# The feed-forwards' first products as seven products of quarters (Strassen), on a two-layer encoder trunk

## The chip, the cores and the metric

One core of one Trainium2 chip runs the whole program in one launch. The metric is the device time of one execution in microseconds (us); the kernel before takes 2049.79 us in the median of 3 runs (2049.25 to 2050.43). A profile of a further execution gives busy time, waits and a timeline for each engine: PE (TensorE matmuls; PEld is its weight load), DVE (VectorE), ACT (ScalarE), POOL (GpSimd) and SP (SyncE, which here issues the loads).

## What is computed

512 frames and 16 learned meta tokens (528 rows of 1024 features) pass through an input LayerNorm and two layers. Each layer has a feed-forward, a mixer and a second feed-forward, each followed by a residual sum and a LayerNorm:

```python
def swiglu_ffn(x, w13, w2):
    a, u = jnp.split(x @ w13, 2, axis=-1)
    return (jax.nn.silu(a) * u) @ w2
for l in range(DEPTH):
    h = layer_norm(DEEPNORM_ALPHA * h + 0.5 * swiglu_ffn(h, ffn1_w13[l], ffn1_w2[l]), ln_g[l, 0], ln_b[l, 0])
    mix = token_mix(h, w_in[l], pool_w[l], pool_scale[l], conv_dw[l], conv_db[l], ...)
    h = layer_norm(DEEPNORM_ALPHA * h + mix, ln_g[l, 1], ln_b[l, 1])
    h = layer_norm(DEEPNORM_ALPHA * h + 0.5 * swiglu_ffn(h, ffn2_w13[l], ffn2_w2[l]), ln_g[l, 2], ln_b[l, 2])
return h[:, N_META:]
```

The hidden width is 2752, that is 21 units of 128 columns and a rest of 64; a unit has a tile of `a` weights and a tile of `u` weights, each 1024 x 128. All data are float32.

## The kernel before

Activations lie transposed: 8 tiles of 128 features, each in two halves of 264 rows (256 frames and 8 meta rows; 256 in the last feed-forward), called s = 0 and s = 1. Each product of float32 numbers is made as three matmuls of a shorter format (`mm3`, lines 101 to 105): every operand is split into a high part, which ACT casts, and a low part, which DVE subtracts (`weights`, lines 82 to 92, for weights; `split`, lines 95 to 99, for activations). The low x low product is left out.

The four feed-forwards are called f0a, f0b, f1a and f1b; the mixers m0 and m1 lie behind f0a and f1a. A feed-forward (`ffn`, and `last_ffn` for f1b) goes through three parts of hidden units (`PARTS`, line 54; the rest of 64 has the number 21). In each part it first makes the hidden units (`hidden_part`, `hidden`): for each unit and each half 8 x 2 `mm3`, then ACT's silu and DVE's product with `u`, and a split. Then comes the second product over that part's units: for each of 8 output tiles m and each half one chain of `mm3` into one PSUM bank, and DVE adds the bank to the residual (`residual`, line 308). In the first part the first three units (`AHEAD`) are done for s = 0 first and for s = 1 after that, since the LayerNorm before them ends earlier for s = 0.

The last part runs inside `normed`: `SKEW` = 6 of the 8 tiles are done for s = 0 and later for s = 1, so that the LayerNorm of s = 0 lies beside the second half of the matmuls, and that of s = 1 beside the next stage's matmuls of s = 0.

Every engine has one queue in order, and a scheduler that is part of the framework fixes that order when the program is built; `issue_after` holds some weights behind the LayerNorm. SP issues all weight loads (512 KB for a 128 x 1024 tile). Buffers are rings: 3 raw weight tiles (`RAW`), 7 high and 7 low ones (`WB`). PSUM has 8 banks: 4 `acc`, 2 `att`, 2 `stat`. POOL does low parts of odd activation tiles, some LayerNorm sums and parts of the mixer; it issues no transfer.

Of the kernel before, what the change touches and what calls it, by code (L numbers as in the profile page):

```python
# [16 lines left out]
P = 128  # L17
D = 1024
# [34 lines left out]

PARTS = ([0, 1, 21, 2, 3, 4], list(range(5, 13)), list(range(13, 21)))


def trunk(ctx, tc, a):
# [43 lines left out]
    def mm3(out, w, x, start, stop):  # L101
        (wh, wl), (xh, xl) = w, x
        nc.tensor.matmul(out, lhsT=wh, rhs=xh, start=start, stop=False)  # L103
        nc.tensor.matmul(out, lhsT=wh, rhs=xl, start=False, stop=False)  # L104
        nc.tensor.matmul(out, lhsT=wl, rhs=xh, start=False, stop=stop)  # L105

# [76 lines left out]
    for tt in range(6):  # L183
        y = wp.tile([P, 1024], F32, tag="hi" if tt % 2 else "lo", name=f"xtok{tt}", bufs=WB)
        tok.append(y[: HM if tt >= 4 else P])

    def load_tokens(tts):
        for tt in tts:
            if tt >= 4:
                nc.sync.dma_start(out=tok[tt], in_=a["meta"][(tt - 4) * HM : (tt - 3) * HM, :])  # L190
                continue
            for c in range(0, D, 512):
                sl = slice(c, c + 512)
                nc.sync.dma_start(out=tok[tt][:, sl], in_=a["x"][tt * P : (tt + 1) * P, sl])

# [246 lines left out]
    def mixer(l, name):  # L442
# [507 lines left out]
```

## Time and profile before

| | us |
|---|---|
| median of 3 runs | 2049.79 |
| profiled execution, its own time | 2050.98 |
| its span, first to last instruction | 2049.2 |
| PE busy | 2001.1 |
| DVE busy | 1055.9 |
| ACT busy | 643.4 |
| POOL busy | 194.1 |

The 16 engines that move data are busy 28.5% of the span with SP's queue and move 178 MB. Of the names in the rows, `f0b_9a_r` is the raw tile of the `a` weights of unit 9 in f0b, `_h` and `_l` its high and low parts, `f0b_9p` the PSUM bank of its products, `f0b_y` a bank of the second product, `m_ln`, `f0b_ln` a LayerNorm behind a mixer or behind f0b. A row of a timeline gives the start, the duration, the engine, the line and the operation.

### The profile page before, as it was taken

The numbers are of one execution on the slowest core, as the hardware profiler recorded it, in microseconds if no ns is written. First come the engines' busy times: TensorE is split into PE (matmuls) and PEld (weight loads), VectorE is DVE, ScalarE is ACT, GpSimd is POOL, SyncE is SP. The second block draws the span as 40 slices with busy tenths as digits, with TensorE's granted clock in tenths as the row PEclk, the third lists the DMA queues.
The fourth block names the chain that finished last, engine by engine and source line by source line (L and its number), as shares of the span: only waits on it lengthen the run. The fifth ranks groups of instructions, "written<-read, shape, count | busy, mean of one in ns | idle before, by whom it ended". The sixth has DMA issues, their size and how long they took to land.

```text
span 2049.2 us, 36659 instructions
## 1 busy us (share of the span) xinstructions
PE 2001.1 (98%) x15344; PEld 1924.7 (94%) x15344; DVE 1055.9 (52%) x2450; ACT 643.4 (31%) x1180; POOL 194.1 (9%) x283
## 2 busy tenths in 40 slices
PE   7999999999999999999999999999999999999997
PEld 6999999997899999999999999999888999998996
DVE  7343333589767443333473433336886683433336
ACT  5322223333324422222262222223333253222230
POOL 4000000340003000000120000004300030000001
PEclk9999999999999999999999999999999999999999
DMA  4432322222211343322233333222222123333231
GB/s 150 132 113 85 99 87 83 74 92 80 63 41 43 97 119 95 93 87 90 64 96 89 101 95 94 89 87 75 71 90 63 42 64 102 96 101 102 84 103 42
DMA packets 54118, 177.98 MB, mean 87 GB/s; under 512 B 6192, under 2 KB 10160, under 8 KB 53952
## 3 DMA queue, kind: packets, MB, share of 16 engines
q1 hardware_dynamic: 52800, 174.59, 28.5%
q8 instruction: 120, 1.97, 0.4%
q10 hardware_dynamic: 1152, 1.05, 0.2%
q14 instruction: 46, 0.38, 0.1%
HBM read 173.52 MB, written 2.10 MB: 86 GB/s over the span
## 4 chain that ended last, share of the span: by engine, by line
PE 84%; DVE 9%; POOL 2%; issue 2%; ACT 1%; DVEq 0%; POOLq 0%; ACTq 0%
PE f1a_y L104 2%; PE f0a_y L104 2%; PE f1a_y L105 2%; PE f1bo L764 2%; PE f1bo L766 2%; PE f0a_y L105 2%; PE f1bo L765 2%; PE f0a_y L103 2%; PE f1a_y L103 2%; PE f0b_y L104 2%; PE f0b_y L105 2%; PE f0b_y L103 2%; DVE m0y L486 1%; DVE m1y L486 1%; PE m1o L614 1%
## 5 line engine op out<-in xcount | busy, mean ns | idle before, releaser
L92 DVE TENSOR_TENSOR f1bw_l<-f1bw_r,f1bw_h 128x512 fp32r<-128x512 f32 x42 | 27.9, 685 | 48.0 <-ACT f1bw_h L89 48.0
L92 DVE TENSOR_TENSOR f0b_o_l<-f0b_o_r,f0b_o_h 128x512 fp32r<-128x512 f32 (+1 forms) x48 | 28.6, 618 | 45.1 <-ACT f0b_o_h L89 45.1
L92 DVE TENSOR_TENSOR f1a_o_l<-f1a_o_r,f1a_o_h 128x512 fp32r<-128x512 f32 (+1 forms) x48 | 28.7, 620 | 45.0 <-ACT f1a_o_h L89 45.0
L92 DVE TENSOR_TENSOR f0a_o_l<-f0a_o_r,f0a_o_h 128x512 fp32r<-128x512 f32 (+1 forms) x48 | 28.6, 618 | 44.8 <-ACT f0a_o_h L89 44.8
L486 DVE SCALAR_TENSOR_TENSOR m1y<-m1u,vec,m1y 128x528 f32<-128x528 f32 x60 | 46.7, 814 | 0.1
L486 DVE SCALAR_TENSOR_TENSOR m0y<-m0u,vec,m0y 128x528 f32<-128x528 f32 x60 | 46.6, 814 | 0.1
L89 ACT CAST f0b_o_h<-f0b_o_r 128x1024 fp32r<-128x1024 f32 (+1 forms) x24 | 22.5, 939 | 55.1 <-PE f0b_y L104 15.6
L89 ACT CAST f1a_o_h<-f1a_o_r 128x1024 fp32r<-128x1024 f32 (+1 forms) x24 | 22.5, 939 | 54.9 <-PE f1a_y L104 15.6
L89 ACT CAST f0a_o_h<-f0a_o_r 128x1024 fp32r<-128x1024 f32 (+1 forms) x24 | 22.5, 938 | 54.7 <-PE f0a_y L104 15.6
L825 POOL TENSOR_TENSOR yt<-yt,g_last 128x256 f32<-128x256 f32 x4 | 3.1, 782 | 346.8 <-ACT yt L824 346.8
L89 ACT CAST f1bw_h<-f1bw_r 128x1024 fp32r<-128x1024 f32 (+1 forms) x22 | 22.2, 1007 | 43.8 <-PE f1bo L766 6.9
L308 DVE TENSOR_TENSOR h<-h,f0b_y 128x264 f32<-128x264 f32 x32 | 13.7, 428 | 41.9 <-PE f0b_y L105 41.9
L308 DVE TENSOR_TENSOR x<-x,f0a_y 128x264 f32<-128x264 f32 x32 | 13.7, 428 | 41.7 <-PE f0a_y L105 41.6
L308 DVE TENSOR_TENSOR h<-h,f1a_y 128x264 f32<-128x264 f32 x32 | 13.7, 427 | 41.7 <-PE f1a_y L105 41.5
L251 POOL TENSOR_TENSOR f0b_ln_s<-h,h 128x264 f32<-128x264 f32 x2 | 1.5, 752 | 324.7 <-DVE h L308 324.7
L251 POOL TENSOR_TENSOR f1a_ln_s<-h,h 128x264 f32<-128x264 f32 x2 | 1.5, 754 | 324.1 <-DVE h L308 324.1
L251 POOL TENSOR_TENSOR f0a_ln_s<-x,x 128x264 f32<-128x264 f32 x2 | 1.5, 758 | 322.3 <-DVE x L308 322.3
L770 DVE TENSOR_TENSOR yt<-yt,f1bo 128x256 f32<-128x256 f32 x48 | 17.2, 417 | 24.8 <-PE f1bo L766 24.8
L104 PE MATMUL m0mo<-m0cat_l,m0wo_h 128*128 128x264 f32 x96 | 27.7, 290 | 0.0
L104 PE MATMUL m1mo<-m1cat_l,m1wo_h 128*128 128x256 f32 x96 | 27.6, 288 | 0.0
L103 PE MATMUL m0mo<-m0cat_h,m0wo_h 128*128 128x264 f32 x96 | 27.4, 288 | 0.0
L105 PE MATMUL m0mo<-m0cat_h,m0wo_l 128*128 128x264 f32 x96 | 27.3, 285 | 0.0
(9053 smaller groups left out, 8847.5 us busy)
## 6 DMA issues: line engine op xcount, KB each, us to landing
f1bw_r<-in_w2last SPq DMA_DIRECT2D x20, 512.0 KB, 4.3
f0a_o_r<-in_w SPq DMA_DIRECT2D x16, 512.0 KB, 4.3
f0b_o_r<-in_w SPq DMA_DIRECT2D x16, 512.0 KB, 3.8
f1a_o_r<-in_w SPq DMA_DIRECT2D x16, 512.0 KB, 4.0
m0wo_r<-in_w_out SPq DMA_DIRECT2D x8, 512.0 KB, 3.5
m1wo_r<-in_w_out SPq DMA_DIRECT2D x8, 512.0 KB, 3.5
m0w_r<-in_w_in SPq DMA_DIRECT2D x6, 512.0 KB, 3.6
m1w_r<-in_w_in SPq DMA_DIRECT2D x6, 512.0 KB, 3.6
```

The lines of the kernel that those rows point to most:

```text
L89: nc.scalar.copy(out=hi[:, :n], in_=w[:, :n])
L92: e.tensor_tensor(out=lo[:, sl], in0=w[:, sl], in1=raw(hi[:, sl]), op=ALU.subtract)
L103: nc.tensor.matmul(out, lhsT=wh, rhs=xh, start=start, stop=False)
L104: nc.tensor.matmul(out, lhsT=wh, rhs=xl, start=False, stop=False)
L105: nc.tensor.matmul(out, lhsT=wl, rhs=xh, start=False, stop=stop)
L308: nc.vector.tensor_tensor(out=y, in0=y, in1=ps, op=ALU.add)
L486: nc.vector.scalar_tensor_tensor(out=ys[c], in0=src, scalar=wk, in1=ys[c], op0=ALU.mult, op1=ALU.add)
L614: nc.tensor.matmul(o[:, c0 : c0 + cw], lhsT=v, rhs=sm, start=i == 0, stop=i == len(sms) - 1)
L764: nc.tensor.matmul(o, lhsT=hh, rhs=wh, start=part > 0 and i == 0, stop=False)
L765: nc.tensor.matmul(o, lhsT=hh, rhs=wl, start=False, stop=False)
L766: nc.tensor.matmul(o, lhsT=hl, rhs=wh, start=False, stop=i == nk - 1)
L770: nc.vector.tensor_tensor(out=y[:, :256], in0=y[:, :256], in1=o, op=ALU.add)
```

## The change

Units 2 to 20 of every feed-forward (19 of 22 entries) no longer take 96 matmuls but 84. The operand is taken as quarters: a11, a12 are feature tiles 0 to 3 and 4 to 7 of half s = 0, a21, a22 those of s = 1; b11, b21 are the two halves of the `a` tile, b12, b22 those of the `u` tile. Seven products of 4 `mm3` replace eight. For these,

- `sums` makes four sums of activations, once in a feed-forward (4 x 4 DVE operations of 128 x 264, and 16 splits);
- `sum_weights` makes, for each unit, t3 = b12 + b22 and t1 = b11 + b12 in place in the raw tiles by transfers that POOL issues and that add while they write, then t2 = t1 + b22 and t4 = t2 + b21 on DVE, and splits all seven operands (seven low parts of 128 x 512 on DVE instead of four);
- `hidden_by_sums` runs the products one after another into two banks, P and Q (and R), adding onto what is there; ACT copies a bank out before the next product is added to it, and DVE combines the copies.

The parts become five: units 0, 1, 21, 2, 3; then three parts of four; then five. `RAW` goes from 3 to 4, `WB` from 7 to 5, the tiles of `hc` from 32 to 20; a new ring of 16 `wide` tiles takes the sums of activations, several mixer tiles and the weights of the last output tiles. `normed` gets `SKEW_F` = 8 in the feed-forwards: all 8 tiles of s = 0, then all of s = 1. The LayerNorm of m1 now keeps its result in `h`, which `sums` reads.

```diff
-TILES = {"x": 32, "h": 16, "hc": 32, "g": 4, "r2": 2, "sm": 5, "s": 2, "q": 4, "dg": 2}
+TILES = {"x": 32, "h": 16, "hc": 20, "g": 4, "r2": 2, "sm": 5, "s": 2, "q": 4, "dg": 2}
-RAW, WB = 3, 7
-SKEW, AHEAD = 6, 3
+RAW, WB, YB = 4, 5, 2
+SKEW, SKEW_F, AHEAD = 6, 8, 3
-PARTS = ([0, 1, 21, 2, 3, 4], list(range(5, 13)), list(range(13, 21)))
+PARTS = ([0, 1, 21, 2, 3], *(list(range(u, u + 4)) for u in (4, 8, 12)), list(range(16, 21)))
...
+    def sums(n, name):
+        out = [[], [], [], []]
+        for i in range(KT // 2):
+            (a11, a21), (a12, a22) = ([y[:, :n] for y in h[m]] for m in (i, i + KT // 2))
+            s1, s2, s3, s4 = (t(f"{name}s{j}{i}", "q" if i % 2 else "sm")[:, :n] for j in range(4))
+            nc.vector.tensor_tensor(out=s1, in0=a21, in1=a22, op=ALU.subtract)
+            nc.vector.tensor_tensor(out=s2, in0=s1, in1=a11, op=ALU.subtract)
+            nc.vector.tensor_tensor(out=s3, in0=a11, in1=a21, op=ALU.subtract)
+            nc.vector.tensor_tensor(out=s4, in0=a12, in1=s2, op=ALU.add)
+            for j, y in enumerate((s1, s2, s3, s4)):
+                out[j].append(split_wide(y, n, f"{name}S{j}{i}"))
+        return out
+
+    def half_split(w, hi, lo, c):
+        sl = slice(c, c + 512)
+        nc.scalar.copy(out=hi[:, sl], in_=w)
+        nc.vector.tensor_tensor(out=lo[:, sl], in0=w, in1=raw(hi[:, sl]), op=ALU.subtract)
+
+    def sum_weights(src, name):
...
+        nc.sync.dma_start(out=wa, in_=src[0])
+        nc.sync.dma_start(out=wu, in_=src[1])
+        b11, b21, b12, b22 = wa[:, :512], wa[:, 512:], wu[:, :512], wu[:, 512:]
+        add = lambda o, y: nc.vector.tensor_tensor(out=o, in0=o, in1=y, op=ALU.add)
+        A, X, U, Y = pair("a"), pair("x"), pair("u"), pair("y", 512, YB)
+        nc.scalar.copy(out=A[0], in_=wa)
+        for c in (0, 512):
+            nc.vector.tensor_tensor(out=A[1][:, c : c + 512], in0=wa[:, c : c + 512], in1=raw(A[0][:, c : c + 512]), op=ALU.subtract)
+        nc.gpsimd.dma_start(out=b12, in_=src[1][:, 512:], accum_op=ALU.add)
+        nc.gpsimd.dma_start(out=b11, in_=src[1][:, :512], accum_op=ALU.add)
+        half_split(b11, *X, 0)
+        nc.scalar.copy(out=U[0], in_=wu)
+        add(b11, b22)
+        half_split(b11, *X, 512)
+        for c in (0, 512):
+            nc.vector.tensor_tensor(out=U[1][:, c : c + 512], in0=wu[:, c : c + 512], in1=raw(U[0][:, c : c + 512]), op=ALU.subtract)
+        add(b21, b11)
+        half_split(b21, *Y, 0)
...
+    def hidden_by_sums(w, S, n, name):
...
+        product(p_, a11, b11, True)
+        m1 = copy(p_, "m1")
+        product(r_, a12, b21, True)
+        nc.vector.tensor_tensor(out=m1, in0=r_[:, :n], in1=m1, op=ALU.add)
+        g0 = t(f"{name}g0", "g")[:, :n]
+        nc.scalar.activation(g0, m1, AF.Silu)
+        product(p_, s2, t2, False)
+        u2 = copy(p_, "u2")
+        product(q_, s1, t1, True)
+        m5 = copy(q_, "m5")
+        product(p_, s3, t3, False)
+        u3 = copy(p_, "u3")
+        nc.vector.tensor_tensor(out=m5, in0=m5, in1=u3, op=ALU.subtract)
+        product(q_, s4, b22, False)
+        nc.vector.tensor_tensor(out=u2, in0=q_[:, :n], in1=u2, op=ALU.subtract)
+        first = gated(g0, u2, 0)
+        product(p_, a22, t4, False)
...
-                normed(KT, step, ns, v, f"{name}_ln", i == 1)
+                normed(KT, step, ns, v, f"{name}_ln", i == 1, SKEW_F)
...
-        normed(KT, step, no, V_LN + (3 * l + 1) * 16, f"{name}_ln", not last)
+        normed(KT, step, no, V_LN + (3 * l + 1) * 16, f"{name}_ln", True, SKEW)
```

Three places of the new order matter below. The first is DVE's queue in f0b where the three plain units (0, 1, 21) end and unit 2 begins. `21h` is the hidden tile of entry 21, `bS` a low part of a sum of activations, `2a` the weights of unit 2. Before:

```order
913 L92 TENSOR_TENSOR f0b_2a_l<-f0b_2a_r,f0b_2a_h 128x512 [waits DMAHW3_49]
914 L291 TENSOR_TENSOR m_ln_x4l<-h_1_7225,m_ln_x4h 128x264 [waits Activation_49]
915 L92 TENSOR_TENSOR f0b_2a_l<-f0b_2a_r,f0b_2a_h 128x512
916 L92 TENSOR_TENSOR f0b_2u_l<-f0b_2u_r,f0b_2u_h 128x512 [waits DMAHW4_49]
917 L92 TENSOR_TENSOR f0b_2u_l<-f0b_2u_r,f0b_2u_h 128x512
918 L291 TENSOR_TENSOR m_ln_x6l<-h_1_7281,m_ln_x6h 128x264 [waits Activation_49]
919 L363 SCALAR_TENSOR_TENSOR f0b_21h_7622<-f0b_21p_0_7596,f0b_21g_7621 64x264 [waits PE_49,Activation_49]
```

Now (`2x` holds t1 and t2 of unit 2, L427 are the two additions, a wait on a name with DMASW is for a transfer of POOL):

```order
1175 L390 SCALAR_TENSOR_TENSOR f0b_21h_8238<-f0b_21p_0_8212,f0b_21g_8237 64x264
1176 L127 TENSOR_TENSOR f0bS_8324<-f0bs_8310,f0bS_8324 128x264 [waits Activation_49]
1177 L431 TENSOR_TENSOR f0b_2a_lo<-f0b_2a_r,f0b_2a_hi 128x512 [waits DMAHW5_49]
1178 L117 TENSOR_TENSOR f0b_21x_l<-f0b_21h_8238,f0b_21x_h 128x264 [waits Activation_49]
1179 L431 TENSOR_TENSOR f0b_2a_lo<-f0b_2a_r,f0b_2a_hi 128x512
1180 L468 TENSOR_TENSOR f0b_2m_8370<-f0b_2R,f0b_2m_8370 128x264 [waits PE_49,Activation_49]
1181 L416 TENSOR_TENSOR f0b_2x_lo<-f0b_2a_r,f0b_2x_hi 128x512 [waits DMASW0_49,Activation_49]
1182 L427 TENSOR_TENSOR f0b_2a_r<-f0b_2a_r,f0b_2u_r 128x512 [waits DMAHW6_49,DVE_49]
1183 L439 TENSOR_TENSOR f0b_2u_lo<-f0b_2u_r,f0b_2u_hi 128x512 [waits DMASW6_49,Activation_49]
1184 L439 TENSOR_TENSOR f0b_2u_lo<-f0b_2u_r,f0b_2u_hi 128x512
1185 L427 TENSOR_TENSOR f0b_2a_r<-f0b_2a_r 128x512 [waits DVE_49]
1186 L416 TENSOR_TENSOR f0b_2x_lo<-f0b_2a_r,f0b_2x_hi 128x512 [waits Activation_49]
```

The low part of unit 2's weights stood ahead of the first product of entry 21 with its gate; now it stands behind all sums and behind the last gate of entry 21.

The second place is ACT's queue while PE does unit 12 of f0b, the first unit of a part. L458 copies a bank out (`12m` from P, then `12u` from P, then `12m` from Q).

```order
777 L429 CAST f0b_13a_hi<-f0b_13a_r 128x1024 [waits DMAHW5_49,PE_49,Activation_49]
778 L415 CAST f0b_12y_hi<-f0b_12a_r 128x512 [waits DVE_49]
779 L458 COPY f0b_12m_10626<-f0b_12P 128x264 [waits PE_49]
780 L415 CAST f0b_13x_hi<-f0b_13a_r 128x512 [waits DMASW5_49,Activation_49]
781 L435 CAST f0b_13u_hi<-f0b_13u_r 128x1024 [waits DMASW3_49,DMAHW6_49,PE_49,Activation_49]
782 L470 ACTIVATE f0b_12g_10641<-f0b_12m_10626 128x264 [waits DVE_49]
783 L458 COPY f0b_12u_10655<-f0b_12P 128x264 [waits PE_49]
784 L415 CAST f0b_13x_hi<-f0b_13a_r 128x512 [waits DVE_49]
785 L429 CAST f0b_14a_hi<-f0b_14a_r 128x1024 [waits DMAHW7_49,PE_49,Activation_49]
786 L458 COPY f0b_12m_10669<-f0b_12Q 128x264 [waits PE_49]
```

Four casts of later units' weights now stand among the copies on which PE's next additions to P and Q wait; before, casts stood there too, but no bank was wanted back within a unit.

The third place is DVE's queue at the same time (`h_1` is the residual of the second product that ends just before unit 12):

```order
1418 L431 TENSOR_TENSOR f0b_13a_lo<-f0b_13a_r,f0b_13a_hi 128x512 [waits DMAHW5_49,Activation_49]
1419 L416 TENSOR_TENSOR f0b_12y_lo<-f0b_12a_r,f0b_12y_hi 128x512 [waits Activation_49]
1420 L335 TENSOR_TENSOR h_1_7776<-h_1_7776,f0b_y_7_1_10569 128x264 [waits PE_49]
1421 L431 TENSOR_TENSOR f0b_13a_lo<-f0b_13a_r,f0b_13a_hi 128x512
1422 L468 TENSOR_TENSOR f0b_12m_10626<-f0b_12R,f0b_12m_10626 128x264 [waits PE_49,Activation_49]
```

The second low part of unit 13's weights, after which POOL may start the adding transfer into b11 of unit 13, stands behind the last residual of the stage before.

## Rows read from the trace of the kernel before

**Rows 1.** The page: busy time of each engine, and granted TensorE clock in 40 slices.
```profile
PE 2001.1 (98%) x15344; PEld 1924.7 (94%) x15344; DVE 1055.9 (52%) x2450; ACT 643.4 (31%) x1180; POOL 194.1 (9%) x283
...
PEclk9999999999999999999999999999999999999999
```
**Rows 2.** Waits of PE: tile, line, what it waited for: us in total, times, longest.
```profile
PE tr L230 <- DVE xtok L215: 11.2, 1, 11.2
...
PE m0sc L595 <- DVE m0sm L606: 4.8, 1, 4.8
...
PE f0b_0p L104 <- DVE m_ln_x6l L291: 1.0, 1, 1.0
```
**Rows 3.** Matmuls of four units: ns min/median/max, then first and last start in us.
```profile
L103 PE MATMUL f0a_5p<-x_h,f0a_5a_h x16: 279/284/286, 122.9 to 133.8; 128*128 128x264 f32 x16
...
L103 PE MATMUL f0a_6p<-x_h,f0a_6a_h x16: 279/284/286, 134.5 to 145.5; 128*128 128x264 f32 x16
...
L103 PE MATMUL f1b_9p<-m_ln_x0h,f1b_9a_h x2: 281/281/281, 1811.3 to 1817.0; 128*128 128x256 f32 x2
...
L103 PE MATMUL f1b_10p<-m_ln_x0h,f1b_10a_h x2: 281/281/281, 1822.6 to 1828.3; 128*128 128x256 f32 x2
```
**Rows 4.** Windows: length, busy us of PE, PEld, DVE, ACT, POOL, clock, DMA share, GB/s.
```profile
495.00:500.00 5.00, 3.64 (x16) 3.65 (x17) 5.00 (x12) 0.06 (x1) 2.21 (x2) 0.50 0.00 0
...
666.00:683.00 17.00, 15.97 (x128) 15.52 (x127) 13.76 (x26) 10.89 (x23) 3.50 (x4) 1.00 0.52 157
766.00:778.00 12.00, 12.00 (x100) 12.00 (x99) 4.32 (x9) 3.40 (x6) 0.00 (x0) 1.00 0.31 89
```
**Rows 5.** Timeline of DVE at the start of f0b: start, us, instruction, count.
```profile
652.30 2.80 DVE L262 TENSOR_TENSOR h<-h,m_ln_mean 128x264 f32<-128x264 f32 x8 [1.23 <-PE m_ln_mean L256]
...
671.04 1.28 DVE L92 TENSOR_TENSOR f0b_2u_l<-f0b_2u_r,f0b_2u_h 128x512 fp32r<-128x512 f32 x2
672.24 0.98 DVE L291 TENSOR_TENSOR m_ln_x6l<-h,m_ln_x6h 128x264 fp32r<-128x264 f32 x1
...
681.64 0.43 DVE L369 SCALAR_TENSOR_TENSOR f0b_1g<-f0b_1p,f0b_1g 128x264 f32<-128x264 f32 x1
```
**Rows 6.** Timeline of ACT at the start of f0b.
```profile
649.63 1.03 ACT L89 CAST f0b_2u_h<-f0b_2u_r 128x1024 fp32r<-128x1024 f32 x1
650.57 0.41 ACT L285 CAST m_ln_x3h<-h 128x264 fp32r<-128x264 f32 x1
...
668.93 0.40 ACT L285 CAST m_ln_x5h<-h 128x264 fp32r<-128x264 f32 x1
669.23 0.52 ACT L288 ACTIVATE m_ln_x6h<-h,vec 128x264 fp32r<-128x264 f32 x1
```
**Rows 7.** Timeline of PE where unit 2 of f0b begins.
```profile
683.17 0.28 PE L103 MATMUL f0b_2p<-m_ln_x0h,f0b_2a_h 128*128 128x264 f32 x1
```
**Rows 8.** DMA issues: KB each, median us from issue to landing.
```profile
m0wo_r<-in_w_out SPq DMA_DIRECT2D x8, 512.0 KB, 3.5
...
f0b_o_r<-in_w SPq DMA_DIRECT2D x8, 320.0 KB, 3.0
...
xtok<-in_x SPq DMA_DIRECT2D x8, 256.0 KB, 5.9
...
out<-yt SPq DMA_DIRECT2D x8, 128.0 KB, 1.8
```
**Rows 9.** Timeline of PE behind the wait in m0.
```profile
496.36 0.79 PE L595 MATMUL m0sc<-m0q00r,m0k00r 128*128 128x128 f32 x2 [4.80 <-DVE m0sm L606]
...
497.17 0.42 PE L104 MATMUL m0gp<-f0a_ln_x2l,m0wg_h 128*128 128x264 f32 x1
497.39 0.42 PE L105 MATMUL m0gp<-f0a_ln_x2h,m0wg_l 128*128 128x264 f32 x1
```
**Rows 10.** Timeline of DVE in f0b's LayerNorm of s = 0: last residual, first scaled tile.
```profile
1015.38 0.43 DVE L308 TENSOR_TENSOR h<-h,f0b_y 128x264 f32<-128x264 f32 x1 [2.49 <-PE f0b_y L105]
...
1031.41 2.09 DVE L281 SCALAR_TENSOR_TENSOR h<-h,vec,f0b_ln_rs 128x264 f32<-128x264 f32 x5 [0.47 <-PE f0b_ln_rs L171]
```

More of the change, by code (lines that the diff above doesn't have):

```diff
@@ L93, in weights, with weights_wide, tile_of @@
         return hi, lo
+    def weights_wide(src, n, name):
+        w = wp.tile([P, 1024], F32, tag="raw", name=f"{name}_r", bufs=RAW)
+        nc.sync.dma_start(out=w[:, :n], in_=src)
+        out = []
+        for c in range(0, n, 512):
+            k = min(512, n - c)
+            hi, lo = (wide(f"{name}_{p_}{c}", F32R) for p_ in "hl")
+            nc.scalar.copy(out=hi[:, :k], in_=w[:, c : c + k])
+            nc.vector.tensor_tensor(out=lo[:, :k], in0=w[:, c : c + k], in1=raw(hi[:, :k]), op=ALU.subtract)
+            out.append((hi, lo))
+        return out
+    def tile_of(w, j):
+        if isinstance(w, list):
+            return at(w[j // 4], slice(j % 4 * P, (j % 4 + 1) * P))
+        return at(w, slice(j * P, (j + 1) * P))
     def split(src, n, name, tag="hc"):
@@ L99, in split, with wide, split_wide, mm3 @@
         return hi, lo
-    def mm3(out, w, x, start, stop):
+    def wide(name, dt=F32):
+        return sq_pool.tile([P, WIDE], dt, tag="wide", name=name, bufs=WIDES)
+    def split_wide(src, n, name):
+        y = wide(name, F32R)
+        hi, lo = y[:, :NT], y[:, NT : 2 * NT]
+        nc.scalar.copy(out=hi[:, :n], in_=src)
+        nc.vector.tensor_tensor(out=lo[:, :n], in0=src, in1=raw(hi[:, :n]), op=ALU.subtract)
+        return hi, lo
+    def mm3(out, w, x, start, stop, onto=False):
         (wh, wl), (xh, xl) = w, x
-        nc.tensor.matmul(out, lhsT=wh, rhs=xh, start=start, stop=False)
-        nc.tensor.matmul(out, lhsT=wh, rhs=xl, start=False, stop=False)
-        nc.tensor.matmul(out, lhsT=wl, rhs=xh, start=False, stop=stop)
+        nc.tensor.matmul(out, lhsT=wh, rhs=xh, start=start, stop=False, skip_group_check=onto)
+        nc.tensor.matmul(out, lhsT=wh, rhs=xl, start=False, stop=False, skip_group_check=onto)
+        nc.tensor.matmul(out, lhsT=wl, rhs=xh, start=False, stop=stop, skip_group_check=onto)
     def at(pair, sl):
@@ L183, in trunk @@
     for tt in range(6):
-        y = wp.tile([P, 1024], F32, tag="hi" if tt % 2 else "lo", name=f"xtok{tt}", bufs=WB)
-        tok.append(y[: HM if tt >= 4 else P])
+        tok.append([wide(f"xtok{tt}{i}")[: HM if tt >= 4 else P, :512] for i in range(2)])
     def load_tokens(tts):
         for tt in tts:
[L189 to L194, printed above, removed]
+            src = a["meta"][(tt - 4) * HM : (tt - 3) * HM] if tt >= 4 else a["x"][tt * P : (tt + 1) * P]
+            for i, y in enumerate(tok[tt]):
+                nc.sync.dma_start(out=y, in_=src[:, i * 512 : (i + 1) * 512])
     rows = [[], []]
@@ L220, in enter @@
         entered["last"] = last.ins
-        rows[s] = [(tok[tt], tok[tt].shape[0]) for tt in group]
+        rows[s] = [(tok[tt], tok[tt][0].shape[0]) for tt in group]
     def turn(s):
@@ L319, in normed @@
         norm_apply(0, ns[0], ra, v, range(4), f"{name}0", keep)
-        for m in range(n - SKEW, n):
+        for m in range(n - skew, n):
             with tc.issue_after(first) if m >= n - LATE else nullcontext():
@@ new lines, in hidden_by_sums, with product, copy, gated @@
+    def hidden_by_sums(w, S, n, name):
+        b11, b21, t1, t2, t3, b22, t4 = w
+        s1, s2, s3, s4 = S
+        a11, a12, a22 = ([xs[m][s] for m in range(k, k + KT // 2)] for k, s in ((0, 0), (KT // 2, 0), (KT // 2, 1)))
+        p_, q_, r_ = acc(f"{name}P"), acc(f"{name}Q"), acc(f"{name}R", "att")
+        def product(o, x, w, first):
+            for i in range(KT // 2):
+                mm3(o[:, :n], at(w, slice(i * P, (i + 1) * P)), at(x[i], slice(0, n)), first and i == 0, i == KT // 2 - 1, True)
+        def copy(o, k):
+            y = t(f"{name}{k}", "sm")[:, :n]
+            nc.scalar.copy(out=y, in_=o[:, :n])
+            return y
+        def gated(g, u, s):
+            nc.vector.scalar_tensor_tensor(out=g, in0=u, scalar=0.5, in1=g, op0=ALU.mult, op1=ALU.mult)
+            return split(g, n, f"{name}x{s}")
+        product(p_, a11, b11, True)
[15 more added lines that the diff above has]
+        product(p_, a22, t4, False)
+        g1 = t(f"{name}g1", "g")[:, :n]
+        nc.scalar.activation(g1, p_[:, :n], AF.Silu)
+        return [first, gated(g1, m5, 1)]
@@ L372, in hidden_part @@
+    summed = {}
     def hidden_part(part, src, ns, name, between={}):
         hid, w = {}, {}
-        for u, s in in_two(PARTS[part], AHEAD if part == 0 else 0, between):
+        plain = PARTS[part][: AHEAD if part == 0 else 0]
+        for u, s in in_two(plain, AHEAD, between):
             if s == 0:
-                i = PARTS[part].index(u)
-                late = part == 0 and "first" in rooted and i >= LATE_W
+                i = plain.index(u)
+                late = "first" in rooted and i >= LATE_W
@@ L381, in hidden_part @@
             hid[u].append(hidden(u, w[u], s, ns[s], f"{name}_{u}"))
+        if part == 0:
+            summed[name] = sums(ns[0], name)
+        for u in PARTS[part][len(plain) :]:
+            with tc.issue_after(rooted["second"]) if plain and "second" in rooted else nullcontext():
+                wu = sum_weights(src["p"][u], f"{name}_{u}")
+            hid[u] = hidden_by_sums(wu, summed[name], ns[0], f"{name}_{u}")
         return hid
@@ L474, in mixer @@
         us, xp = ([seq[kind, c] for c in range(2)] for kind in ("u", "xp"))
-        ys = [sq_pool.tile([P, L], F32, tag="y", name=f"{name}y{c}", bufs=2) for c in range(2)]
+        ys = [wide(f"{name}y{c}")[:, :L] for c in range(2)]
         def conv_taps():
```

38 lines of the change are left out of this document (23 added, 15 removed).

## The prediction

> **What bounds the kernel now.** I read the page first: PE is busy 2001.1 of 2049.2 us, at the full granted clock in every slice, while DVE is busy 52% and ACT 31% [rows 1]. The waits of PE come next: the longest is one of 11.2 us at the start, one of 4.8 us in each mixer follows, and the waits at the starts of the feed-forwards are of about 1 us; no wait inside a unit is listed [rows 2]. So what a matmul less is worth is the pitch of matmuls: the tiles of units 5 and 6 start 11.6 us apart for 96 matmuls, 0.1208 us each (0.28 us is the duration of one, which overlaps the next); in the last feed-forward, with 256 columns, 11.3 us or 0.1177 [rows 3]. Third, the windows show how much room the helpers have: in the middle of a part DVE is busy 4.3 and ACT 3.4 of 12 us, but at the start of f0b DVE is busy 13.8 of 17 [rows 4]. The change takes work from PE and gives it to DVE, ACT and POOL, so it is at these two places that it has to be followed. I sum against the profiled execution, 2051.0 us, which lies 1.2 above the median.
>
> **What it removes.** 12 matmuls in each of 19 units of three feed-forwards: 684 x 0.1208 = 82.6 us; 228 x 0.1177 = 26.8 in f1b; 9 more fall away because the last part there is shorter, 1.1. Together **-110.5 us**, all on PE's path. The order agrees: 15008 rows of PE become 14087. The page "TensorE: Matmul & The Clock Gate" of the Trainium skill (Back-to-back issue gap) gives N/2.4 + 2.5 ns, 112.5 ns for 264 columns, where the trace shows 120.8; by the page the gain would be some 103 us and the time about 7 us higher. The trace decides.
>
> **Whether DVE or ACT becomes the bound.** Per unit DVE does nine operations of 128 x 512 (seven low parts, two additions) and seven of 128 x 264. Queued, these take 0.60 and 0.34 us (2.80 us for eight, 1.28 for two [rows 5]): 9 x 0.60 + 7 x 0.34 = 7.8 us. ACT casts 2 x 0.94, 3 x 0.5 (half of a cast of 1024, an estimate) and eight tiles of 264 at 0.30 [rows 6]: 5.8 us. PE needs 84 x 0.1208 = 10.2. Neither is the bound, even if each DVE operation paid its single duration (0.68 and 0.43: 9.1 us). The 76 units move 76 x 512 KB = 40 MB more; moving 178 MB takes 28.5% of the transfer engines, so some 35%: hidden. The 32 more residual additions of 0.43 us in a feed-forward lie beside second products in which DVE has about half its time free (11.7 of 23.2 us: eight times two additions and one low part); without that cover they would cost 14 us each time. What costs is order and latency, at three kinds of places.
>
> **The unknown price.** The adding transfer of 256 KB, issued by POOL, is in no row. Call L the time from the end of DVE's last low part of the `a` weights to its landing. From below: a plain transfer of 128 KB lands after 1.8 us and one of 320 KB after 3.0, so 256 KB after about 2.6. If reading the destination counts as moving 512 KB, 3.5; the slowest median of 256 KB, in the crowd at the start, is 5.9 [rows 8]. I take **L = 3.0**, between the plain transfer and the one of 512 KB, and keep 2.6 and 5.9 as ends. The page "DMA: Bandwidth & Descriptors" (Anatomy of one DMA, SWDGE path) gives 2.0 us + bytes/436e3 for a plain transfer from GpSimd, 2.6 us; by that figure the sum below would come to about 2010. No row here shows it.
>
> **Start of a feed-forward.** Plain units end at 683.17 in f0b [rows 7]. In the 17 us before, DVE had 13.8 us of work, ten low parts of units 2 to 4 (6.2) in it. They go; 32 operations for the sums come (32 x 0.34 = 10.9) and one low part must follow them (0.6), since the order puts unit 2's weights behind the sums: 13.8 - 6.2 + 11.5 = 19.1, 2.1 us over; with 1.6 us of the idle 3.2 remaining (waits for ACT's casts and for gates, such as the one at 681.64 [rows 5]) unit 2 starts 3.7 us late. The low part of a LayerNorm tile that PE waits for before that (672.24) stays where it is. Then unit 2's third product needs t2. Its chain starts at the end of the second low part, 0.9 us after the first: L, cast and low part of t1 (1.3), addition (0.6), two low parts of u (1.3), addition and low part (1.3): L + 4.5, while PE has two products (2.9 us): a stall of L + 2.5 = 5.5, the 0.9 counted. Unit 3, prepared in the same haste, adds 0.1. So 9.3 us, four times: **+37**. After an idle of 4.8 us in m0 the granted clock is 0.50 [rows 4], and matmuls start 0.22 us apart instead of 0.12 for some 4.5 us behind it [rows 9], half of which, 2.2 us, is lost. The stall here is as long, so +2.2 each, **+9**.
>
> **Inside the parts.** ACT's queue decides here. Let unit 12's first product start at 0. DVE's last low part of unit 13's `a` stands behind the residual of the stage before: 0.2 (end of the last matmul) + 0.43 + 0.6 = 1.3. The transfer lands at 1.3 + L = 4.3. ACT waits for it with the cast of `13x` (to 4.8), casts `13u` (to 5.8), silu (6.1), and only then copies u2 out of P (6.5), which PE wants back for its fifth product at 4 x 1.45 = 5.8: 0.8 late with an issue gap. A half and a whole cast stand before the copy of Q: 0.3 more. In the next two units the transfer is in time at L = 3.0, but casts of 1024 before u2 and m5 leave 0.2 to 0.3 at each of three copies. Sum 1.9 us a part; 4 parts in 4 feed-forwards: **+30**. Each us of L more costs 1 here, 1 at the next unit (its first copy) and about half at the third. Part 0 is in the starts.
>
> **Ends of parts and LayerNorms.** The last unit's low part comes about 0.3 us after PE wants it (1.3 us for silu, gate, cast and low part, against 9 matmuls): 20 x 0.3 = **+6**. With `SKEW_F` the cover of the LayerNorm of s = 0 is 8 x 15 x 0.1208 = 14.5 us, where six tiles of 24 matmuls gave 17.4; in f0b it took 16.0 from the last residual to the first scaled tile [rows 10], and the first low part comes 1 us later: 2.5 us late, three times, **+8**. The smaller ring of weights (5 instead of 7) I cost at nothing in the mixers: five tiles are what their first three jobs hold, and raw tiles go from 3 to 4. Without that cover a job would wait for one cast and two low parts, 2.2 us.
>
> **Sum.** 2051.0 - 110.5 + 37 + 9 + 30 + 6 + 8 = 2030.5; as a median **2029 us**. One us of L moves it by 4 x 2 + 16 x 2.5 = 48.
>
> **Rivals.** (1) *The helpers stay ahead.* The walk through the queues gives each cast its place in time from few rows; if copies find ACT free and LayerNorms keep their cover, only the starts cost: 2049.8 - 110.5 + 46 = 1985. For it: DVE has 2.4 and ACT 4.4 us to spare in each unit. Against it: the order, in which casts that wait for transfers stand ahead of copies. (2) *Slower: the adding transfer is slow.* Mechanism: ACT sits at the cast behind it, the copies come late, PE waits for its banks in every unit. From L = 3.4 the time is that of before; at L = 4.2 it is 2029 + 1.2 x 48 = 2087, at 5.9 some 2170. For it: POOL's issue and the second reading are in no row, and loads of 512 KB run beside it. (3) *The starts alone give the gain back*, without a slow transfer, if the sums wait longer for casts: each us is 4 us; it would take 5 us more at each to reach the old time. I count it in the band of no change.
>
> **How the numbers follow.** Forecast, 2005 to 2045: 0.35. Rival 1, 1975 to 2005: 0.25. Between 2045.7 and 2053.9, within 0.2% (about what a measurement of this kernel can tell from no change): 0.08. Rival 2: 0.32, of which 0.14 beyond 2090. So faster 0.60, same 0.08, slower 0.32. The range 1975 to 2090 leaves out 0.14 above and 0.06 below; the forecast's own range is 2005 to 2045.
>
> **What would show it.** PE's matmuls 921 fewer at the same pitch. Its waits: at unit 2 of each feed-forward two, some 3.7 us for the low part of 2a and 5.5 for 2x, with the clock at 0.50 behind them; in units 4, 8, 12 and 16 waits of about 1 us for ACT's copies. The new transfers' issue to landing near 3 us; above 3.5 the forecast falls to rival 2, and if the listed waits inside units are missing, to rival 1. DVE near 75% of the span. Wrong would also be a matmul pitch that changes, or a wait in a mixer.

## The result, and the profile after

| | before | after |
|---|---|---|
| median, us | 2049.52 (2048.08 to 2050.43, 4 runs) | 2168.35 (2166.41 to 2171.36, 4 runs) |
| ratio, 95% interval | | 1.0582 (1.0563 to 1.0600) |
| profiled execution, its span | 2050.98, 2049.2 | 2171.36, 2169.6 |

The change is slower by 119 us, where some 20 less was forecast. The matmuls fell by the 921 that the order said (110 us), so PE lost some 230 us elsewhere. The page after, against [rows 1] (the queues q1 and q0 are those of SP and of POOL):

```profile
PE 1976.1 (91%) x14423; PEld 1868.9 (86%) x14423; DVE 1473.5 (68%) x3314; ACT 906.5 (42%) x1845; POOL 346.8 (16%) x435
...
PEclk9999999999999999999999999999999999999998
...
q1 hardware_dynamic: 59744, 174.59, 25.6%
q0 software_dynamic: 21888, 39.86, 11.8%
```

No engine is full: PE is idle 9%, DVE 32%, ACT 58%. POOL's queue takes 11.8% of the transfer engines for 39.9 MB, SP's 25.6% for 174.6 MB: a byte that is added costs twice the engines' time of a loaded one. PE's waits (tile, line, what it waited for, us, times, longest) answer to [rows 2], where no wait stood inside a unit:

```profile
PE f0b_y L133 <- DVE h L335: 6.5, 3, 2.8
...
PE f0b_12P L133 <- ACT f0b_12u L458: 5.5, 1, 5.5
...
PE f0b_2P L135 <- DVE f0b_2a_lo L431: 2.8, 1, 2.8
...
PE f1b_14P L133 <- ACT f1b_14m L458: 1.8, 1, 1.8
```

The wait of 5.5 us stands in units 4, 8, 12 and 16 of three feed-forwards (4.5 to 5.6; 3.0 in f0b's unit 16). What it does to the clock is seen in the windows of 5 us (PE, PEld, DVE, ACT and POOL busy, then the granted clock, DMA share, GB/s), as in [rows 4]:

```profile
935.00:940.00 5.00, 4.50 (x37) 4.23 (x35) 3.15 (x7) 0.90 (x2) 0.87 (x1) 1.00 0.70 165
940.00:945.00 5.00, 0.01 (x1) 0.01 (x1) 1.53 (x3) 2.21 (x5) 0.86 (x1) 0.86 0.54 107
945.00:950.00 5.00, 5.00 (x23) 5.00 (x23) 4.48 (x8) 2.73 (x5) 0.86 (x1) 0.50 0.65 157
```

After the idle stretch the clock is at 0.50 (1.2 GHz), and 23 matmuls run in 5 us where 41 would.

For the whole feed-forwards I added up the distances between starts in PE's timeline, above 0.1215 us each, with a wait and without one (the half clock, mostly):

| where | waits, us | half clock, us | forecast |
|---|---|---|---|
| units 2 and 3 | 24.9 | 15.0 | 37 + 9 |
| first unit of a part | 66.6 | 29.3 | with the two rows below, 30 |
| second unit of a part | 10.4 | 4.8 | |
| other units | 30.1 | 5.7 | |
| second products | 18.4 | 11.8 | 6 |

That is 217 of the 230 us. The starts came near the forecast; the units inside the parts lost 147 us where 30 were forecast, the second products 30 where 6 were. All but 5 of the 96 us at first units lie in f0a, f0b and f1a.

### The profile page after: what moved, and what is told of

The parts are those of the page before. It is cut to its first block, busy times and chain, and to the rows that moved or that the text cites. A ratio compares the mean times of both kernels' runs of the same rounds, so it can differ in the third digit from the quotient of the medians.

```text
span 2169.6 us, 37210 instructions
## 1 busy us (share of the span) xinstructions
PE 1976.1 (91%) x14423; PEld 1868.9 (86%) x14423; DVE 1473.5 (68%) x3314; ACT 906.5 (42%) x1845; POOL 346.8 (16%) x435
## 3 DMA queue, kind: packets, MB, share of 16 engines
q1 hardware_dynamic: 59744, 174.59, 25.6%
q0 software_dynamic: 21888, 39.86, 11.8%
q10 hardware_dynamic: 1152, 1.05, 0.1%
## 4 chain that ended last, share of the span: by engine, by line
PE 48%; DVE 16%; DMA 16%; issue 9%; ACT 8%; POOL 3%; SPq 0%; ACTq 0%; POOLq 0%; DVEq 0%
PE f1bo L890 1%; PE f1bo L888 1%; PE f1bo L889 1%; DVE m1y L610 1%; PE f0a_y L134 1%; PE f0a_y L133 1%; PE f0a_y L135 1%; PE f1a_y L134 1%; DVE m0y L610 1%; PE f0b_y L134 1%; PE f1a_y L133 1%; PE f0b_y L133 1%; PE f1a_y L135 1%; PE f0b_y L135 1%; PE m0sc L719 1%
## 5 line engine op out<-in xcount | busy, mean ns | idle before, releaser
L335 DVE TENSOR_TENSOR h<-h,f1a_y 128x264 f32<-128x264 f32 x64 | 27.2, 426 | 27.9 <-PE f1a_y L135 27.7
L335 DVE TENSOR_TENSOR x<-x,f0a_y 128x264 f32<-128x264 f32 x64 | 27.2, 426 | 27.2 <-PE f0a_y L135 27.1
L335 DVE TENSOR_TENSOR h<-h,f0b_y 128x264 f32<-128x264 f32 x64 | 27.1, 425 | 27.1 <-PE f0b_y L135 26.9
L91 ACT CAST f1a_o_h<-f1a_o_r 128x512 fp32r<-128x512 f32 (+1 forms) x37 | 23.5, 636 | 45.1 <-PE f1a_y L134 29.0
L91 ACT CAST f0b_o_h<-f0b_o_r 128x512 fp32r<-128x512 f32 (+1 forms) x37 | 23.5, 636 | 44.9 <-PE f0b_y L134 29.0
L91 ACT CAST f0a_o_h<-f0a_o_r 128x512 fp32r<-128x512 f32 (+1 forms) x37 | 23.5, 635 | 44.4 <-PE f0a_y L134 28.9
L94 DVE TENSOR_TENSOR f0a_o_l<-f0a_o_r,f0a_o_h 128x512 fp32r<-128x512 f32 (+1 forms) x42 | 26.6, 642 | 10.4 <-ACT f0a_o_h L91 7.8
L291 ACT ACTIVATE m_ln_q<-h 128x264 f32<-128x264 f32 (+1 forms) x32 | 11.9, 414 | 39.7 <-DVE h L289 36.2
L281 POOL TENSOR_TENSOR m_ln_s<-m_ln_s,h 128x264 f32<-128x264 f32 (+1 forms) x20 | 18.6, 928 | 31.4 <-DVE h L329 25.5
L134 PE MATMUL m0mo<-m0cat,m0wo_h 128*128 128x264 f32 x64 | 18.4, 289 | 0.0
L134 PE MATMUL m1mo<-m1cat,m1wo_h 128*128 128x256 f32 x64 | 18.3, 287 | 0.0
L133 PE MATMUL m0mo<-m0cat,m0wo_h 128*128 128x264 f32 x64 | 18.3, 288 | 0.0
```

The costliest lines, as they stand in the source:

```text
L91: nc.scalar.copy(out=hi[:, :n], in_=w[:, :n])
L94: e.tensor_tensor(out=lo[:, sl], in0=w[:, sl], in1=raw(hi[:, sl]), op=ALU.subtract)
L335: nc.vector.tensor_tensor(out=y, in0=y, in1=ps, op=ALU.add)
```

## One part of the loss, followed through the queues

Unit 12 of f0b, whose ACT and DVE queues the order showed. POOL's timeline in the change (L432 issues t3's transfer, L433 t1's):

```profile
923.58 0.86 POOL L432 DMA_DIRECT2D f0b_13u_r<-in_w13p  x1 [6.56 <-DMA f0b_13u_r<-in_w13p]
924.86 0.88 POOL L433 DMA_DIRECT2D f0b_12a_r<-in_w13p  x1 [0.42 <-issue]
936.56 0.87 POOL L433 DMA_DIRECT2D f0b_13a_r<-in_w13p  x1 [10.82 <-DVE f0b_13a_lo L431]
```

DVE's, with the low parts of `12a` and `13a` (two each), behind which t1's transfers may start:

```profile
920.51 0.69 DVE L431 TENSOR_TENSOR f0b_12a_lo<-f0b_12a_r,f0b_12a_hi 128x512 fp32r<-128x512 f32 x1 [0.58 <-ACT f0b_12a_hi L429]
...
921.46 0.68 DVE L431 TENSOR_TENSOR f0b_12a_lo<-f0b_12a_r,f0b_12a_hi 128x512 fp32r<-128x512 f32 x1
...
923.88 0.43 DVE L335 TENSOR_TENSOR h<-h,f0b_y 128x264 f32<-128x264 f32 x1 [1.02 <-PE f0b_y L135]
930.60 0.69 DVE L416 TENSOR_TENSOR f0b_12x_lo<-f0b_12a_r,f0b_12x_hi 128x512 fp32r<-128x512 f32 x1 [6.30 <-ACT f0b_12x_hi L415]
931.21 0.42 DVE L335 TENSOR_TENSOR h<-h,f0b_y 128x264 f32<-128x264 f32 x1
...
935.58 0.68 DVE L431 TENSOR_TENSOR f0b_13a_lo<-f0b_13a_r,f0b_13a_hi 128x512 fp32r<-128x512 f32 x1
...
937.13 0.68 DVE L431 TENSOR_TENSOR f0b_13a_lo<-f0b_13a_r,f0b_13a_hi 128x512 fp32r<-128x512 f32 x1
```

ACT's:

```profile
919.43 1.05 ACT L429 CAST f0b_12a_hi<-f0b_12a_r 128x1024 fp32r<-128x1024 f32 x1 [2.30 <-PE f0b_y L134]
929.95 0.62 ACT L415 CAST f0b_12x_hi<-f0b_12a_r 128x512 fp32r<-128x512 f32 x1 [9.47 <-DMA f0b_12a_r<-in_w13p]
...
932.79 1.04 ACT L429 CAST f0b_13a_hi<-f0b_13a_r 128x1024 fp32r<-128x1024 f32 x1
...
942.79 0.62 ACT L415 CAST f0b_13x_hi<-f0b_13a_r 128x512 fp32r<-128x512 f32 x1 [6.53 <-DMA f0b_13a_r<-in_w13p]
943.31 1.04 ACT L435 CAST f0b_13u_hi<-f0b_13u_r 128x1024 fp32r<-128x1024 f32 x1
944.26 0.42 ACT L470 ACTIVATE f0b_12g<-f0b_12m 128x264 f32<-128x264 f32 x1
944.58 0.36 ACT L458 COPY f0b_12u<-f0b_12P 128x264 f32<-128x264 f32 x1
```

And PE's:

```profile
931.69 0.39 PE L133 MATMUL f0b_y<-f0b_8x_h,f0b_o_h 128*128 128x264 f32 x1 [2.01 <-DVE h L335]
...
933.33 0.36 PE L133 MATMUL f0b_12P<-m_ln_x0h,f0b_12a_hi 128*128 128x264 f32 x1
...
945.00 0.59 PE L133 MATMUL f0b_12P<-f0bS,f0b_12u_hi 128*128 128x264 f32 x1 [5.50 <-ACT f0b_12u L458]
```

The first low part of `12a` ends at 921.20, the second at 922.14. POOL issues t1's transfer only at 924.86, because t3's of unit 13 stands ahead in its queue and waits for its load to land (in most other first units the profile puts that wait down to a residual of DVE). t1's transfer lands at 929.9. ACT has stood at its cast for 9.5 us, DVE behind ACT for 6.3, and behind DVE's low part stand the residuals that free the banks, so PE waits 2.0 us already in the second products. The cast of `13a`, behind all this in ACT's queue, comes at 932.79, and its first low part, behind what DVE has to make up, at 935.58; so unit 13's transfer is issued at 936.56, lands 6.1 later, and the copy of `12u`, which PE wants at 939.5, stands behind that too.

One reading ahead of the prediction was wrong: POOL does not wait for the second low part of a unit's weights. Unit 13's transfer is issued at 936.56, 0.3 us behind the first low part, and the second starts only at 937.13; the transfer overwrites the half that the first has read. In 63 of the 76 units it was issued before the second had ended. In f0a, f0b and f1a POOL held the first units' transfers for 1.8 to 4.0 us behind the first low part, in f1b for 0.3 us, where first units lose little; f1b's second products differ as well, so this alone does not show the cause.

## Experiments

Theory A: the wait is for the transfer behind t1, at the head of ACT's and DVE's queues. Theory B: the load on DVE and ACT. Theory C: the frame (parts, rings, `SKEW_F`). Times are medians; ratios are to the kernel before, with 95% intervals. "L" is the time from the end of DVE's last low part of `a` to the start of the cast that waits, as the median over the 16 first, the 16 second and the 36 other units behind part 0; in the change 7.4, 4.9 and 4.1 us. Where L is compared over the units, it is added up unit by unit over these 68.

**The frame alone, all units plain.**

```diff
-        plain = PARTS[part][: AHEAD if part == 0 else 0]
-        for u, s in in_two(plain, AHEAD, between):
+        plain = PARTS[part]
+        for u, s in in_two(plain, AHEAD if part == 0 else 0, between):
...
-        if part == 0:
-            summed[name] = sums(ns[0], name)
```

> All units keep the 96 matmuls of before (no sums, no adding transfers); the five parts, the smaller rings and SKEW_F of the change stay. Theory A (the adding transfer behind t1 lands 4 to 6 us after its issue, and ACT and DVE stand still at the cast behind it): the frame costs little, 2050 to 2075 us, and PE has no wait over 3 us in a part. Theory C (the frame itself, the parts and the rings, makes the loss): 2110 us or more.

2056.29 us, 1.0028 (1.0017 to 1.0040). The frame costs 6 us; theory C falls. My terms for it (ends of parts 6, LayerNorms 8) came to 14, more than twice that.

**Plain transfers from POOL.** They move the same bytes to the same places, and t1 and t3 are not formed: the kernel leaves out these two additions.

```diff
-        nc.gpsimd.dma_start(out=b12, in_=src[1][:, 512:], accum_op=ALU.add)
-        nc.gpsimd.dma_start(out=b11, in_=src[1][:, :512], accum_op=ALU.add)
+        nc.gpsimd.dma_start(out=b12, in_=src[1][:, 512:])
+        nc.gpsimd.dma_start(out=b11, in_=src[1][:, :512])
```

> POOL's transfers no longer add, they write the same 256 KB plainly (t1 and t3 are left out of the computation, which becomes copies of quarters of the weights). If the second reading of the destination is what makes the transfer slow, its median from issue to landing falls from 4.4 to about 3 us, and by 48 us for each us the time falls to about 2100 (2080 to 2125). If the price is that of any transfer that POOL issues among SP's loads, landing stays at 4 us or more and the time above 2145. Theory B (the load on DVE and ACT, not the wait): unchanged, 2160 to 2175.

2069.43 us, 1.0096 (1.0081 to 1.0111). Issue to landing of t1's 76 transfers (min, median, max), in the change

```profile
DMA to landing us min/median/max: 3.7/4.7/6.9
```

and with plain writes

```profile
DMA to landing us min/median/max: 2.9/3.4/5.3
```

The adding itself costs 1.3 us in the median of t1's transfers (1.1 in that of t3's), and nothing else was changed: 99 us. L fell to 4.2, 3.4 and 3.2, in all by 88 us: some 1.1 us of time for each us of L. By the Trainium skill's page "DMA: Bandwidth & Descriptors" (Anatomy of one DMA, SWDGE path) a plain 256 KB takes an estimated 2.6 us; the least of these, beside other loads, is 2.9.

**t1 made by DVE.**

```diff
-        nc.gpsimd.dma_start(out=b11, in_=src[1][:, :512], accum_op=ALU.add)
-        half_split(b11, *X, 0)
         nc.scalar.copy(out=U[0], in_=wu)
-        add(b11, b22)
+        add(b11, b12)
         half_split(b11, *X, 512)
...
         add(b21, b11)
+        nc.vector.tensor_tensor(out=b11, in0=b11, in1=b22, op=ALU.subtract)
+        half_split(b11, *X, 0)
```

> t1 without a transfer: t3 is still made by the first adding transfer, then DVE makes t2 = b11 + t3 and t1 = t2 - b22 in place, one operation of 128 x 512 more in each unit. Theory A: the waits of 5 us at P in the first unit or two of a part, the ones of 2 to 3 us for residuals, and the half clock behind them go; 2000 to 2060 us. Theory B (load on DVE and ACT): DVE has 76 x 0.6 = 46 us more to do, and the time stays above 2140.

1993.31 us, 0.9718 (0.9698 to 0.9737): faster than before, and 175 us better than the change, though DVE does more.

```profile
PE 1911.4 (96%) x14423; PEld 1822.3 (92%) x14423; DVE 1512.8 (76%) x3390; ACT 919.8 (46%) x1845; POOL 284.4 (14%) x359
```

DVE is busy 39 us more than in the change. Theory B falls. No wait at the first unit of a part is left; the largest in f0b is that at unit 2 (2.8 us, as in the change). The four executions lie between 1986 and 1995 us, more apart than those of the other kernels. The edit also puts the cast of t1 behind the other operands', so it takes away the wait and moves the cast.

**Both additions on POOL itself.** In the change's two lines `nc.gpsimd.tensor_tensor` takes the place of `nc.gpsimd.dma_start`; t1 is now added first, since t3 overwrites its operand.

> t1 and t3 as two additions of 128 x 512 on POOL itself in place of the two adding transfers, in the same places of the program. By its 0.93 us for 128 x 264 one should take about 1.8 us, against 4 to 6 for the transfer. Theory A: 1990 to 2060 us. Theory B: 2140 or more. If the additions on POOL hold up DVE's own, DVE's operations of 128 x 512 get longer than 0.69 us and the time lies between.

2024.42 us, 0.9874 (0.9858 to 0.9891). It lies between, as the last sentence expected. Low parts on DVE and the addition on POOL in unit 12 of f0b (ns min/median/max, first and last start):

```profile
L431 DVE TENSOR_TENSOR f0b_12a_lo<-f0b_12a_r,f0b_12a_hi x2: 691/1180/1668, 856.0 to 856.9; 128x512 fp32r<-128x512 f32 x2
...
L432 POOL TENSOR_TENSOR f0b_12a_r<-f0b_12a_r,f0b_12u_r x1: 1298/1298/1298, 856.8 to 856.8; 128x512 f32<-128x512 f32 x1
```

The low part that starts beside POOL's addition takes 1.67 us instead of 0.69 and ends 0.5 us behind it; DVE's busy time rises by 93 us with the same operations. The Trainium skill's page "SBUF — State Buffer" (SBUF: two separate sides) says that a DVE operation with two SBUF inputs and a GpSimd one that reads SBUF exclude each other for a whole instruction; this row agrees.

**t3 on DVE too, and t3 alone.** The lines with `b12` become `add(b12, b22)`, on top of e3 or of the change.

> As e3_t1_dve, and t3 too is added by DVE: no adding transfer is left, DVE does eleven operations of 128 x 512 in a unit. If t3's transfers were harmless in e3 (they start when the raw tile lands, long before anyone wants them), the time stays within 10 us of e3's 1993; if the transfers as such cost something (traffic, POOL's issues), it falls below 1980; if DVE's load now counts, it rises above 2005.

1981.58 us, 0.9667 (0.9653 to 0.9681): 12 us better than e3, between the two bounds set; t3's transfers cost little where nobody waits for t1's, and DVE's further 76 operations nothing that shows.

> The other half of e3: t1 stays an adding transfer, t3 is added by DVE. Theory A (only the transfer that waits for DVE's last low part, and for which ACT waits in turn, costs): 2110 to 2160 us, near the change's 2168, the rest being POOL's queue, in which t1 of a part's first unit stood behind the next unit's t3. Rival (each of the two transfers costs about half): 2070 to 2095.

2123.65 us, 1.0357 (1.0340 to 1.0374). So with both transfers 2168, t3's removed 2124, t1's removed 1993, none 1982: t1's is the main cause (142 us without t3's), and t3's makes it worse.

**POOL's queue.**

```diff
-        nc.gpsimd.dma_start(out=b12, in_=src[1][:, 512:], accum_op=ALU.add)
-        nc.gpsimd.dma_start(out=b11, in_=src[1][:, :512], accum_op=ALU.add)
+        with tc.issue_after(added["t1"]) if added else nullcontext():
+            nc.gpsimd.dma_start(out=b12, in_=src[1][:, 512:], accum_op=ALU.add)
+        added["t1"] = nc.gpsimd.dma_start(out=b11, in_=src[1][:, :512], accum_op=ALU.add).ins
```

> The change as it was, but t3's transfer of a unit is held behind the t1 transfer of the unit before in POOL's queue. If the 45 us that e6 gained over the change came from POOL's queue (t1 of a part's first unit behind t3 of the next), t1 there is issued 1 to 3 us earlier, in 16 parts less the first of each feed-forward: about 16 x 2 = 30 us, 2130 to 2150. If they came from the traffic and POOL's issues of t3 themselves, no change: 2160 to 2180.

2104.55 us, 1.0265 (1.0251 to 1.0279). The gain is 64 us, twice what I expected, with every transfer still there. POOL's timeline here (t1's is L436, t3's L435):

```profile
888.85 0.86 POOL L436 DMA_DIRECT2D f0b_12a_r<-in_w13p  x1 [4.68 <-DVE f0b_12a_lo L433]
890.69 0.88 POOL L435 DMA_DIRECT2D f0b_13u_r<-in_w13p  x1 [0.98 <-issue]
```

Unit 12's transfer goes first, and it also lands sooner. From issue to landing the 12 first units of f0a, f0b and f1a take 4.0 us in the median, in the change 5.7; there an adding transfer of t3 had been issued 0.5 to 0.6 us ahead (1.3 in the unit followed above). L is 3.5, 3.9 and 4.1, in all 58 us less than in the change, and the time is 64 less: 1.1 for each us again. The gain is also more than the 45 us of e6, which has no transfer of t3 but one more operation on DVE in each unit; what makes this difference, no run separates.

**The same transfers, later in ACT's queue.** The cast and low parts of U stand ahead of `half_split(b11, *X, 0)`:

```diff
+        nc.scalar.copy(out=U[0], in_=wu)
+        for c in (0, 512):
+            nc.vector.tensor_tensor(out=U[1][:, c : c + 512], in0=wu[:, c : c + 512], in1=raw(U[0][:, c : c + 512]), op=ALU.subtract)
         half_split(b11, *X, 0)
-        nc.scalar.copy(out=U[0], in_=wu)
         add(b11, b22)
         half_split(b11, *X, 512)
-        for c in (0, 512):
-            nc.vector.tensor_tensor(out=U[1][:, c : c + 512], in0=wu[:, c : c + 512], in1=raw(U[0][:, c : c + 512]), op=ALU.subtract)
```

> The same operations and transfers as the change, written in another order: the cast and the low parts of the u tile come ahead of the cast that waits for the transfer behind t1. The scheduler then also moves casts behind the copies of banks. Theory A: the transfer takes as long as before (4 to 6 us), but more stands ahead of the cast that waits for it; at some 50 to 80 us for each us of wait, 2060 to 2120 us. Theory B, or if only the chain's length counts and not what stands behind the cast in the queues: 2150 to 2175.

2080.26 us, 1.0148 (1.0133 to 1.0163), with L as in the change: 7.4, 4.7 and 4.2. ACT's timeline:

```profile
885.26 1.05 ACT L434 CAST f0b_12u_hi<-f0b_12u_r 128x1024 fp32r<-128x1024 f32 x1 [1.87 <-PE f0b_y L134]
892.75 0.62 ACT L415 CAST f0b_12x_hi<-f0b_12a_r 128x512 fp32r<-128x512 f32 x1 [6.44 <-DMA f0b_12a_r<-in_w13p]
...
903.01 0.62 ACT L415 CAST f0b_13x_hi<-f0b_13a_r 128x512 fp32r<-128x512 f32 x1 [4.84 <-DMA f0b_13a_r<-in_w13p]
903.54 0.42 ACT L470 ACTIVATE f0b_12g<-f0b_12m 128x264 f32<-128x264 f32 x1
903.86 0.36 ACT L458 COPY f0b_12u<-f0b_12P 128x264 f32<-128x264 f32 x1
```

The cast of `u`, of 1.05 us, now stands ahead of the cast that waits, in all 76 units, and the copy comes 0.9 us behind the cast of `13x` instead of 1.8. ACT's idle time before these casts, where a transfer ended it, added over the units behind part 0, falls from 252 to 144 us. So it is not the transfer's length alone that costs, but what stands behind it in a queue.

**Without the starts, and the best.** `plain = PARTS[part] if part == 0 else []` makes units 2 and 3 plain, on e3 and on e5.

> e3_t1_dve with units 2 and 3 of each feed-forward made plainly (96 matmuls), so that unit 4 is the first that needs the sums of activations, with a whole stage of second products for them. It costs 96 matmuls more, 11.6 us; if the starts of feed-forwards cost the 8 to 10 us each that the waits at unit 2 and the half clock behind them show in e3, they go: 1970 to 1985 us. If the stall only moves to unit 4, 2000 to 2010.

1975.26 us, 0.9635 (0.9621 to 0.9650).

> e5_dve_all and the plain units 2 and 3 of e7 together: no adding transfer, no sums needed before unit 4. If the two gains are of separate places they add up: 1981.6 - 18 = 1963 us (1958 to 1970). If DVE, now with eleven wide operations in each of 17 units, binds, above 1972.

1968.16 us, 0.9602 (0.9589 to 0.9615): it gains 13 us on e5 where e7 gained 18 on e3; e3's executions lie too far apart to read anything from the difference. In the last, unit 3 moves out of part 0:

```diff
-PARTS = ([0, 1, 21, 2, 3], *(list(range(u, u + 4)) for u in (4, 8, 12)), list(range(16, 21)))
+PARTS = ([0, 1, 21, 2], list(range(3, 7)), list(range(7, 11)), list(range(11, 16)), list(range(16, 21)))
```

> e9 with unit 3 moved out of the plain part: parts of 4, 4, 4, 5 and 5 entries, 48 matmuls fewer in all, 5.8 us. The sums must be ready one unit earlier, but a stage of second products still lies between. 1954 to 1962 us if nothing else moves; above e9 if two parts of five units in a row wait for the ring of hidden tiles.

**1962.62 us, 0.9574 (0.9561 to 0.9587)**, the fastest: 87 us below before, 206 below the change, just above the range expected.

```profile
PE 1911.4 (97%) x14471; PEld 1827.8 (93%) x14471; DVE 1529.6 (78%) x3450; ACT 906.6 (46%) x1819; POOL 210.9 (11%) x283
```

## Why the prediction was wrong

- *What it removes* (-110.5 us) held. Where the waits are gone it shows: e10 has 15344 - 14471 = 873 matmuls less than before [rows 1], at 0.1208 us 105 us, and is 87 us faster, the frame's 6 among the difference. The 112.5 ns that the prediction took from the Trainium skill's page "TensorE: Matmul & The Clock Gate" (Back-to-back issue gap) is there the gap of an isolated matmul; the stream of weight loads and matmuls here starts them 120.8 ns apart [rows 3].
- *Whether DVE or ACT becomes the bound* held: DVE 68%, and e3 and e5 load it more and are faster.
- *The unknown price* failed. I took **L = 3.0** for every unit, the time of a plain transfer of 320 KB [rows 8]. The adding transfer alone takes at least 3.7 us from issue to landing, 4.7 in the median, and L is 7.4, 4.9 and 4.1, 5.0 in the mean. That is nearer to the crowded 256 KB [rows 8], 5.9, which I kept as the far end. For the 512 KB that a second reading would make I took 3.5, a row of a mixer. In the feed-forwards, where the loads stand, such loads took 3.8 to 4.3 on the profile's page of before:

```profile
f0a_o_r<-in_w SPq DMA_DIRECT2D x16, 512.0 KB, 4.3
f0b_o_r<-in_w SPq DMA_DIRECT2D x16, 512.0 KB, 3.8
```

- *Inside the parts* failed with it: 30 us forecast, 147 measured. At the first unit of each part I had 1.1 us of wait; 4.2 us were measured and 1.8 more of half clock. I started the walk at unit 12's first product, with unit 12's own weights ready, and had unit 13's transfer land 4.3 us behind that. In the trace it lands 9.4 us behind it (942.7 against 933.33): 1.9 us of the difference come from a later issue, 3.1 from a longer transfer. The issue is late because the wait begins before the walk does, when POOL holds t1 of unit 12 behind t3 of unit 13. The order as I read it showed no such row, since I read ACT and DVE there and not POOL's queue. e11 prices that at 64 us. Counting L from the second low part, where POOL waits only for the first, was an error the other way: it made the forecast later.
- *Ends of parts*: the residuals behind `12x`'s low part (18 us of waits, 12 of half clock) were in no term.
- *Slope*: I had 48 us for each us of L, 0.63 for each of 76 units; e2 and e11 give about 1.1 for each of 68. From e2's L down to 3.0 is 45 us over these units, times 1.1 is 50: an estimate of some 2020 us at the L that I assumed, against 2029. By that estimate the rest of the sum stood, and the size put into it did not.
- *Starts*: 40 us against 46, fewer of them waits and more of them half clock. *LayerNorms and rings*: 8 and nothing, where the whole frame costs 6 (e1), so no loss was hidden there.
- *Rivals*: the second happened. Its price at 5.9, "some 2170", came out almost to the us, but by chance: L was 5.0 in the mean, and the slope steeper. I gave it 0.32 and only 0.14 beyond 2090, because I weighed the middle of the range and not the place where the transfers crowd. The chances also do not add up: forecast, rival 1, no change and rival 2 make 1.00, which leaves nothing for the 0.06 below 1975.

## What to carry to other kernels

A transfer whose issue waits for a computation and whose result is waited for at once is best kept off the path of the busiest engine. If it must stand there, price it by the slowest row of its size, from the place where the loads stand, and read the issuing engine's queue too. An in-order engine should not meet a wait for a transfer ahead of work that PE needs; if such work stands behind it, move the work ahead (88 us here) or make the operand by an engine (175 us). DVE's idle time, 32% of the span, paid for that at no cost that shows.

## What was not expected of the hardware

A transfer that adds took 1.3 us longer than a plain one of the same 256 KB and twice the share of the transfer engines for each byte (q0 moved the same 39.86 MB with 5.8% in e2, 11.8% in the change). One issued 0.5 to 0.6 us behind another (1.3 in one unit) took 5.7 us to land, in the median of twelve, instead of 4.0 in e11. Plain loads beside it went with as long a time: unit 13's, with two loads of 512 KB issued 1.8 us ahead of it and 0.3 us behind it, took 6.1. POOL's own part of an issue rose from 0.54 to 0.86 us.
